# A diffusion block on one core: tables in the slots of split weights, four slots of each kind, and the last attention head inside the output projection

## The chip, the cores and the metric

The kernel runs on one NeuronCore of a Trainium2 chip. The metric is the device time of one execution in microseconds (us). TensorE (PE) does the matmuls, VectorE (DVE) and ScalarE (ACT) the elementwise work, GpSimd (POOL) a few elementwise steps, and SyncE (SP) issues most DMAs. Each engine works through its own instructions in a fixed order and waits for the others by semaphores.

## The reference

Two streams of 256 tokens with 1024 channels, the latent stream `lat` and the context stream `cx`, pass through two layers. Each layer is a gated feed-forward block (ffn), a mixer and a second ffn; each of them reads a normed and modulated copy of the stream (`adaln_in`) and adds its result to it through a gate. The mixer of layer 0 is the one that the change touches:

```python
def macaron(h, gain, mod, k, w1, w3, w2):
    return h + 0.5 * mod[:, 3*k+2] * swiglu(adaln_in(h, gain, mod, k), w1, w3, w2)

# layer 0: mixer_ab
u = h @ w_in                                # q, k, v of 4 heads, and 3 x 512 channels for hyena
a = head_out(diff_attend(q, k_all, v_all, lam))   # two softmaxes a head, subtracted, then rmsnorm
b = hyena(u[..., 3 * A_WIDTH:])             # short convolution, then two long ones by FFT, each gated
y = concatenate([a, b], axis=-1) @ w_out    # 512 channels of each
```

Layer 1 has neighbourhood attention with 16 heads in its place. All of it is float32.

## The kernel before

**Matmuls in three parts.** Every operand of a matmul is split into a high part `h` in fp32r and the rest `l`; `mm3` (L161 to L164) adds three matmuls, high by high (L162), high by low (L163) and low by high (L164). A piece of weights is 128x1024 elements: `whalf` takes one slot of tag `whi` and one of tag `wlo` in the pool `wp` and calls `split` (L156), in which ACT writes the high part (L158) and DVE, or POOL where it is asked for, subtracts it for the low part (L159). So a piece is there once both have run, and its two slots come free when the last matmul that reads them is done. The pool holds three slots of each tag; the raw weights come by DMA into `raw`, three slots too.

**Where pieces stand in line.** A block of an ffn needs four pieces: two of `w1` and two of `w3`. `ffn` begins with `ffn_first`, which asks for all four at once and puts the low parts on POOL (on DVE in the very first ffn, whose pieces are made early); `products` then runs them over stream 0 and, when it is normed, over stream 1. `project_first` does the same at the start of a mixer, with four pieces in `mixer_ab`, by DVE. With three slots the fourth piece waits until the first is read for the last time. All other places (`project`, `project_v`, `out_project`, the later blocks of an ffn) use pieces by twos.

**Norms.** Before each block a stream's statistics go squares on ACT, six adds on DVE (L448), four matmuls (L452, L453), a power on POOL (`rs`, L456), a broadcast by matmul (L464), then `xr` and `h` on DVE and ACT (L491 to L493).

**mixer_ab.** It loads three tables of the Fourier transforms, each 128 x 2 x 512 (4 KB a partition, the size of one slot of a piece), into a pool `tb` of their own. `project` runs over the channels of `w_in`, two pieces at a time; `step()` pulls the next part of the generator `convolutions` between them. `head(hd)` does one attention head: scores (L752), two softmaxes for each half of the queries (`softmax_exp`, then L758), transposes of the result on PE (L677), and the product with the values (`pu<-ah,v`). For stream 0 a score is 512 wide, for stream 1 256 wide. `conv2` (`ps<-tab,y`) ends the convolution and fills `zb`, four tiles. `norms` norms two heads: squares, L903, a power on POOL (`rs16`, L907), L912, and `za`, the tiles `z`. Then `out_project` adds the product with `w_out`: eight blocks of output from `zb` (96 matmuls 512 wide, `pd<-zb`), and then the same from `za` (`pd<-z`).

**Order.** The order of each engine's instructions is fixed when the program is built, by a list scheduler; a pool's slots enter it as dependencies: a tile can be written only after the last reader of the tile that had its slot. So the order of the code sets priorities, and the number of slots sets what may run early.

Of the kernel before, what the change touches and what calls it, by code (L numbers as in the profile page):

```python
# [18 lines left out]
P = 128  # L19
# [85 lines left out]
def tile_dit(ctx: ExitStack, tc: tile.TileContext, a: dict, out: bass.AP, dbg=None):  # L105
# [1 line left out]
    dbg = dbg or {}  # L107

    const = ctx.enter_context(tc.tile_pool(name="const", bufs=1))
    wp = _Pool(ctx.enter_context(tc.tile_pool(name="wp", bufs=3)))  # L110
    hp = _Pool(ctx.enter_context(tc.tile_pool(name="hp", bufs=8)))
    gp = _Pool(ctx.enter_context(tc.tile_pool(name="gp", bufs=10)))
    mp = _Pool(ctx.enter_context(tc.tile_pool(name="mp", bufs=6)))
    fp = _Pool(ctx.enter_context(tc.tile_pool(name="fp", bufs=3)))
    tb = _Pool(ctx.enter_context(tc.tile_pool(name="tb", bufs=3)))
    tp = _Pool(ctx.enter_context(tc.tile_pool(name="tp", bufs=NT)))
    xp = _Pool(ctx.enter_context(tc.tile_pool(name="xp", bufs=6)))
    sp = _Pool(ctx.enter_context(tc.tile_pool(name="sp", bufs=2)))
# [392 lines left out]
    def gates(l, i, half):  # L511
        g = sp.tile([P, 8, 2], F32, tag="gate", name="gate")
        V.tensor_scalar(g, modT[l][:, 8 * i : 8 * i + 8, :], 0.5 if half else 1.0, None, op0=ALU.mult)
        return g
# [173 lines left out]
    def mixer_ab(ad, mods, after):  # L688
# [49 lines left out]
        def head(hd):  # L738
            (qh, ql), (kh, kl) = qk[hd], qk[4 + hd]
            if hd % 2 == 0:  # L740
                oT[hd], oT[hd + 1] = G(F32, "oT")
            for s in range(2):
                nk = 4 if s == 0 else 2
                n = P * nk
                at = [PS() for _ in range(nk // 2)]
                for qt in range(2):
                    qs = slice(LAT * s + P * qt, LAT * s + P * qt + P)
                    pss = [PU(), PU()]
                    for i in range(3):
                        for m in range(2):  # L750
                            pr = slice(64 * m, 64 * m + 64)
                            nc.tensor.matmul(pss[m][:, :n], (qh, qh, ql)[i][pr, qs], (kh, kl, kh)[i][pr, TOK - n :],  # L752
                                             start=i == 0, stop=i == 2)
                    e0, s0 = softmax_exp(pss[0], n)
                    e1, s1 = softmax_exp(pss[1], n)
                    V.tensor_tensor(s1[:, 3:4], s1[:, 2:3], nlam, op=ALU.mult)
                    S.activation(e1[:, :n], e1[:, :n], AF.Copy, scale=s1[:, 3:4])
                    V.scalar_tensor_tensor(e0[:, :n], e0[:, :n], s0[:, 2:3], e1[:, :n], op0=ALU.mult, op1=ALU.add)  # L758
                    transposed(at, e0, nk, qt)
                po = PU()  # L760
                hs = slice(P * hd, P * hd + P)
                weighted(po, at, nk, lambda kt: [x[:, hs] for x in vs[kt + 4 - nk]])
                S.activation(oT[hd][:, LAT * s : LAT * s + LAT], po[:, :LAT], AF.Copy)
# [126 lines left out]
        def step(n=1):  # L890
            for _ in range(n):
                next(hyena, None)
# [3 lines left out]
        def norms(hds):  # L896

            st = PS()
            for i, hd in enumerate(hds):
                q = T(name="sq")  # L900
                S.activation(q, oT[hd], AF.Square)
                for t in range(4):
                    nc.tensor.matmul(st[:, 4 * i + t : 4 * i + t + 1], q[:, P * t : P * t + P], ones, start=True, stop=True)  # L903
            n = 4 * len(hds)
            rs = sp.tile([P, 16], F32, tag="rs16", name="rs16")
            V.tensor_scalar(rs[:, :n], st[:, :n], 1.0 / P, EPS, op0=ALU.mult, op1=ALU.add)
            nc.gpsimd.tensor_tensor(rs[:, :n], rs[:, :n], nhalf[:, :n], op=ALU.pow)  # L907
            for i, hd in enumerate(hds):
                bc = PS()
                for t in range(4):  # L910
                    k = 4 * i + t
                    nc.tensor.matmul(bc[:, P * t : P * t + P], rs[:, k : k + 1].to_broadcast([P, P]), ident, start=True, stop=True)  # L912
                x = T(name="on")
                V.scalar_tensor_tensor(x, oT[hd], sub8, bc, op0=ALU.mult, op1=ALU.mult)
                za.append(G(name="z"))
                split(*za[hd], x)

        tab = [tb.tile([P, 2, TOK], F32R, tag="tb", name="tab") for i in range(3)]
        tables(0, 3, lambda i: tab[i][:, 0], lambda i: tab[i][:, 1])
        tabs = [[tab[0][:, x].rearrange("p (i t f) -> p i t f", i=2, t=2)[:, i] for x in range(2)] for i in range(2)]  # L920
        inv = [[[tab[1 + f][:, x, LAT * i : LAT * i + LAT] for x in range(2)] for i in range(2)] for f in range(2)]
# [14 lines left out]
        project_v(win, 1280, h, emit_v(1), PD)  # L936
        step(2)
        head(2)
        step()
        head(3)  # L940
        step(99)
        norms((2, 3))
        gate = gates(0, 5, False)
        out_project(wout, range(4, 8), [(x[:, 0], x[:, 1]) for x in zb], gate, [0, 1])
        mods(-1)
        out_project(wout, range(4), za, gate, [0, 1], None, after)

    def mixer_c(ad, mods, after):
# [174 lines left out]
    def mods(ns, first=None, until=None):  # L1123

        def f(b, part=0):
            if b < 0:
                if first:
                    mod_until(*first)  # L1130
            elif b < NFB - 2:
                mod_some(ns[part])
            elif b == NFB - 2 and until and part == 3:
                mod_until(*until)
        return f
# [47 lines left out]
```

## Time and profile before

| what | value |
|---|---|
| median of 3 runs | 1936.07 us (1931.74 to 1936.6) |
| the profiled execution | 1930.48 us, span 1928.7 us |
| PE busy | 1845.0 us, 96% of the span |
| DVE busy | 1281.3 us, 66% |
| ACT busy | 732.4 us, 38% |
| POOL busy | 91.1 us, 5% |
| PE's mean granted clock | 0.98 of full speed |

The profile gives the busy time of each engine, with matmuls counted from start to modelled end, and PE's granted clock. There are two levels of it, 2.4 GHz (1.0) and 1.2 GHz (0.5). A 128x512 matmul that stands in a row follows the last by about 0.23 us at the full level, a 128x256 one by 0.12 us, and by twice that at the lower level. The span falls into an opening of 60 us, the first ffn (to about 445 us), `mixer_ab` (to about 745), two ffns (to 1130 and 1510), layer 1's mixer (to about 1720) and the last ffn.

### The profile page before, as it was taken

How to read it: one execution, taken by the hardware profiler on the slowest of the kernel's cores; microseconds unless marked ns; L12 is line 12 of the kernel's file. 1: busy time of each engine (PE TensorE's matmuls, PEld its weight loads, DVE VectorE, ACT ScalarE, POOL GpSimd, SP SyncE). 2: the span in 40 equal slices, each digit the busy share in tenths (PEclk: the TensorE clock that was granted, in tenths of full speed). 3: DMA queues.
4: the chain of work that ended last, by engine and by line, in shares of the span. 5: the costliest groups of instructions: out<-in, count | busy, mean ns of one | idle time of the engine just before them, and what ended most of it. 6: DMA issues, size and time to landing. Idle time of an engine off the chain costs nothing.

```text
span 1928.7 us, 25545 instructions
## 1 busy us (share of the span) xinstructions
PE 1845.0 (96%) x10250; PEld 1561.9 (81%) x10250; DVE 1281.3 (66%) x2007; ACT 732.4 (38%) x1191; POOL 91.1 (5%) x91
## 2 busy tenths in 40 slices
PE   7899999998998888999999999999999999979998
PEld 3678788888887667878888888888888988879998
DVE  5567686677898656677767467566334866667675
ACT  4333233234454433422322333223212566644444
POOL 1000000000101002000000010000000101110000
PEclk9999999999999889999999999999999999989999
DMA  8664455451332111555545315434323233325552
GB/s 282 223 228 175 144 217 178 141 185 47 119 99 66 55 44 44 189 182 186 175 153 177 129 45 202 169 142 141 100 88 114 78 83 104 83 88 204 182 184 88
DMA packets 182791, 266.63 MB, mean 138 GB/s; under 512 B 19026, under 2 KB 133973, under 8 KB 182673
## 3 DMA queue, kind: packets, MB, share of 16 engines
q1 hardware_dynamic: 179128, 256.35, 39.7%
q0 software_dynamic: 2288, 6.53, 1.0%
q10 hardware_dynamic: 1256, 2.13, 0.3%
q8 instruction: 80, 1.31, 0.3%
q14 instruction: 39, 0.31, 0.0%
HBM read 259.74 MB, written 5.24 MB: 137 GB/s over the span
## 4 chain that ended last, share of the span: by engine, by line
PE 56%; DVE 2%; ACT 1%; POOL 1%; issue 1%; DVEq 0%; POOLq 0%; ACTq 0%
PE pu L164 11%; PE pu L162 10%; PE pu L163 10%; PE pd L162 5%; PE pd L163 5%; PE pd L164 5%; PE ps L162 2%; PE ps L164 2%; PE ps L163 2%; PE pu L1034 1%; POOL wl L159 1%; DVE acc L448 1%; PE pu L1004 1%; PE ps L307 1%; ACT wh L158 0%
## 5 line engine op out<-in xcount | busy, mean ns | idle before, releaser
L164 PE MATMUL pu<-h,wl 128*128 128x512 f32 (+1 forms) x1600 | 549.1, 344 | 15.6 <-POOL wl L159 10.9
L162 PE MATMUL pu<-h,wh 128*128 128x512 f32 (+1 forms) x1600 | 548.7, 345 | 6.5 <-ACT h L492 3.1
L163 PE MATMUL pu<-h,wh 128*128 128x512 f32 (+1 forms) x1600 | 548.6, 343 | 0.2 <-DVE h L493 0.2
L158 ACT ACTIVATE wh<-raw 128x1024 fp32r<-128x1024 f32 x228 | 241.2, 1059 | 598.1 <-PE pu L163 403.0
L159 DVE TENSOR_TENSOR wl<-raw,wh 128x1024 fp32r<-128x1024 f32 x216 | 264.1, 1224 | 171.9 <-ACT wh L158 170.9
L164 PEld LDWEIGHTS pu<-h,wl 128*128 128x128 f32 x1600 | 307.4, 192 | 51.7 <-POOL wl L159 11.8
L162 PEld LDWEIGHTS pu<-h,wh 128*128 128x128 f32 x1600 | 306.5, 192 | 51.4 <-ACT wh L158 8.0
L163 PEld LDWEIGHTS pu<-h,wh 128*128 128x128 f32 x1600 | 307.7, 192 | 35.2 <-issue 0.8
L296 DVE SCALAR_TENSOR_TENSOR mv<-mw,kept,mv 128x1024 f32<-128x1024 f32 x210 | 258.2, 1278 | 2.6 <-DMA mw<-in_mod_w_dram 2.6
L556 DVE TENSOR_TENSOR sg<-sg,pu 128x512 f32<-128x512 f32 (+1 forms) x87 | 52.5, 604 | 173.0 <-PE pu L164 153.9
L158 ACT ACTIVATE w<-raw 128x1024 fp32r<-128x1024 f32 x88 | 90.9, 1055 | 188.8 <-PE ps L163 110.5
L519 DVE SCALAR_TENSOR_TENSOR kept<-pd,gate,kept 128x256 f32<-128x256 f32 x244 | 110.5, 478 | 58.8 <-PE pd L164 58.4
L159 DVE TENSOR_TENSOR w<-raw,w 128x1024 fp32r<-128x1024 f32 x88 | 106.6, 1221 | 43.4 <-ACT w L158 43.1
L162 PE MATMUL pd<-g,w 128*128 128x512 f32 (+1 forms) x376 | 133.2, 354 | 0.0
L164 PE MATMUL pd<-g,w 128*128 128x512 f32 (+1 forms) x376 | 132.2, 352 | 0.0
L163 PE MATMUL pd<-g,w 128*128 128x512 f32 (+1 forms) x376 | 132.2, 352 | 0.0
L162 PE MATMUL ps<-g,w 128*128 128x512 f32 (+1 forms) x320 | 116.1, 363 | 0.0
L164 PE MATMUL ps<-g,w 128*128 128x512 f32 (+1 forms) x320 | 116.0, 363 | 0.0
L163 PE MATMUL ps<-g,w 128*128 128x512 f32 (+1 forms) x320 | 116.0, 363 | 0.0
L162 PE MATMUL pd<-h,wh 128*128 128x512 f32 (+1 forms) x288 | 108.3, 376 | 2.3 <-ACT bo L423 1.2
L163 PE MATMUL pd<-h,wh 128*128 128x512 f32 (+1 forms) x288 | 107.3, 372 | 0.0
L164 PE MATMUL pd<-h,wl 128*128 128x512 f32 (+1 forms) x288 | 107.2, 372 | 0.0
(284 smaller groups left out, 2724.0 us busy)
## 6 DMA issues: line engine op xcount, KB each, us to landing
raw<-in_ffn_w_dram SPq DMA_DIRECT2D x132, 1024.0 KB, 5.3
mw<-in_mod_w_dram SPq DMA_DIRECT2D x144, 512.0 KB, 5.8
raw<-in_ab_w_in_dram SPq DMA_DIRECT2D x12, 1024.0 KB, 4.9
raw<-in_na_w_in_dram SPq DMA_DIRECT2D x12, 1024.0 KB, 5.9
raw<-in_ab_w_out_dram SPq DMA_DIRECT2D x4, 1024.0 KB, 5.9
raw<-in_na_w_out_dram SPq DMA_DIRECT2D x4, 1024.0 KB, 5.0
bias<-in_na_rpb_dram SPq DMA_DIRECT2D x32, 96.0 KB, 6.2
raw<-in_x_dram SPq DMA_DIRECT2D x1, 1024.0 KB, 5.1
```

The costliest lines, as they stand in the source:

```text
L158: S.activation(hi, src, AF.Copy)
L159: eng.tensor_tensor(lo, src, hi.bitcast(F32), op=ALU.subtract)
L162: nc.tensor.matmul(ps, wh, xh, start=start, stop=False)
L163: nc.tensor.matmul(ps, wh, xl, start=False, stop=False)
L164: nc.tensor.matmul(ps, wl, xh, start=False, stop=stop)
L296: V.scalar_tensor_tensor(acc, mw, c, acc, op0=ALU.mult, op1=ALU.add)
L307: nc.tensor.matmul(ps[32 * j : 32 * j + 32], row[:, 31 - b : 63 - b], mod_acc[l, i][j % 2][:, j // 2], start=b == 0, stop=b == len(batch) ...
L448: V.tensor_tensor(acc, acc, q, op=ALU.add)
L519: V.scalar_tensor_tensor(res[d][:, sl], ps[:, po], g[:, d, s : s + 1], res[d][:, sl], op0=ALU.mult, op1=ALU.add)
L556: V.tensor_tensor(sg[:, sl], sg[:, sl], p3[:, sl], op=ALU.mult)
L1004: nc.tensor.matmul(pss[m], x[pr, qsl], y[pr], start=n == 0, stop=n == 2)
L1034: nc.tensor.matmul(po[:, LAT * m : LAT * m + LAT], w, x[:, sl], start=kt == 0 and n == 0, stop=kt == 3 and n == 1)
```

## The change

- The pool `wp` gets four slots of `whi` and four of `wlo` in place of three and three (`raw` keeps three).
- The pool `tb` is gone. The three tables take slots of `wp`: `tab[0]` one of `whi`, `tab[1]` and `tab[2]` two of `wlo`. From the loading of the tables until the last matmul of `conv2` three slots of `whi` and two of `wlo` are left to the weights.
- At the end of `mixer_ab` the last parts of the convolution are pulled before head 3, and head 3 is written between the two halves of the projection of `zb`, in a function that `out_project` calls after each half (`b or head(3)` runs it after the first). `norms((2, 3))` comes after that projection. `mods(-1)`, which does nothing here, is dropped.

```diff
-    wp = _Pool(ctx.enter_context(tc.tile_pool(name="wp", bufs=3)))
+    wp = _Pool(ctx.enter_context(tc.tile_pool(name="wp", bufs=4)))
...
-    tb = _Pool(ctx.enter_context(tc.tile_pool(name="tb", bufs=3)))
...
-        tab = [tb.tile([P, 2, TOK], F32R, tag="tb", name="tab") for i in range(3)]
+        tab = [wp.tile([P, 2, TOK], F32R, tag=("whi", "wlo", "wlo")[i], name="tab") for i in range(3)]
...
         step(2)
         head(2)
-        step()
-        head(3)
         step(99)
+        gate = gates(0, 5, False)
+        out_project(wout, range(4, 8), [(x[:, 0], x[:, 1]) for x in zb], gate, [0, 1], lambda b: b or head(3))
         norms((2, 3))
-        gate = gates(0, 5, False)
-        out_project(wout, range(4, 8), [(x[:, 0], x[:, 1]) for x in zb], gate, [0, 1])
-        mods(-1)
         out_project(wout, range(4), za, gate, [0, 1], None, after)
```

A line of the changed kernel has the number before less one (L752 becomes L751, L677 becomes L676, `mm3` L161 to L163).

PE, the first two softmaxes of head 3, that is its scores 512 wide (`pu<-qk`) and the transposes that wait for the softmaxes (`ps<-kept,e`). In the kernel before PE has the end of the scores, four of twelve matmuls of `zb`, and the transposes:

```order
L162 MATMUL pd<-zb,wh 128x512
L163 MATMUL pd<-zb,wh 128x512
L752 MATMUL pu<-qk 128x512 x6
L164 MATMUL pd<-zb,wl 128x512
L162 MATMUL pd<-zb,wh 128x512
L163 MATMUL pd<-zb,wh 128x512
L164 MATMUL pd<-zb,wl 128x512
L677 MATMUL ps<-kept,e 128x128 x8
```

In the changed kernel PE has at the same place:

```order
L162 MATMUL pd<-zb,wh 128x512
L163 MATMUL pd<-zb,wl 128x512
L751 MATMUL pu<-qk 128x512 x11
L676 MATMUL ps<-kept,e 128x128 x8
L161 MATMUL pu<-ah,v 128x256
L751 MATMUL pu<-qk 128x256 x6
```

Before, the twelve matmuls of `zb` stood among the scores and ahead of the transposes; now they, and the rest of `conv2`, stand ahead of the scores, and the transposes follow the scores directly.

PE, the second two softmaxes of head 3 (scores 256 wide) and their transposes. In the kernel before:

```order
L752 MATMUL pu<-qk 128x256 x6
L677 MATMUL ps<-kept,e 128x128 x2
L752 MATMUL pu<-qk 128x256 x3
L162 MATMUL ps<-tab,y 128x256
L163 MATMUL ps<-tab,y 128x256
```

In the changed kernel PE has, behind 36 matmuls of `zb` that follow the six scores shown above:

```order
L162 MATMUL pd<-zb,wh 128x512
L163 MATMUL pd<-zb,wl 128x512
L163 MATMUL pu<-ah,v 128x256
L676 MATMUL ps<-kept,e 128x128 x2
L751 MATMUL pu<-qk 128x256 x6
L161 MATMUL pd<-zb,wh 128x512
L162 MATMUL pd<-zb,wh 128x512
```

Here the transposes stood right behind the scores, and now 36 matmuls of `zb` stand between; 19 more stand ahead of the next transposes. In all 84 of the 96 matmuls of `zb` stand behind the first transposes of head 3, as before, but behind them all come the norm's L902 (L903 before), six matmuls of `z`, and the norm's L911 (L912 before), where 70 matmuls of `zb` stood behind L912.

DVE, the start of `mixer_ab`: `h` of stream 1 for its last two blocks of channels, then low parts of weights (`wl`), and `cv`, the short convolution of the first results. In the kernel before the low part here, `wl_3546`, is the fourth piece's (the third's, `wl_3542`, stands 69 rows above):

```order
L493 SCALAR_TENSOR_TENSOR h_3354<-xr_3489,kept_96,h_3354 128x256
L493 SCALAR_TENSOR_TENSOR h_3359<-xr_3493,kept_96,h_3359 128x256
L159 TENSOR_TENSOR wl_3546<-raw_3539,wh_3545 128x1024
L777 SCALAR_TENSOR_TENSOR cv_3745<-pu_3549,kept_96,cv_3745 128x2x255
L777 SCALAR_TENSOR_TENSOR cv_3762<-pu_3550,kept_96,cv_3762 128x2x255
```

In the changed kernel DVE has `wl_3539`, the third piece's, and `wl_3543`, the fourth's:

```order
L492 SCALAR_TENSOR_TENSOR h_3351<-xr_3486,kept_93,h_3351 128x256
L492 SCALAR_TENSOR_TENSOR h_3356<-xr_3490,kept_93,h_3356 128x256
L158 TENSOR_TENSOR wl_3539<-raw_3536,wh_3538 128x1024
L158 TENSOR_TENSOR wl_3543<-raw_3536,wh_3542 128x1024
L776 SCALAR_TENSOR_TENSOR cv_3742<-pu_3546,kept_93,cv_3742 128x2x255
```

The third piece's low part has moved from the time before stream 1's norm to behind it, next to the fourth's. On PE 46 matmuls of stream 0 stand ahead of stream 1's L451 there, where 72 stood ahead of L452. On POOL the order of the four low parts ahead of the second ffn and the norms' powers was one, `rs`, two, `rs`, one, and is two, `rs`, two, `rs`; and on PE 66 matmuls of that ffn's first block stand ahead of the broadcast L463 of stream 1, where 51 stood ahead of L464.

## Rows read from the trace of the kernel before

**Rows 1.** Windows, columns in the first row: an ffn's steady blocks, then `mixer_ab`.

```profile
core 0: us, PE busy (x) PEld busy (x) DVE busy (x) ACT busy (x) POOL busy (x), PEclk, DMA share, GB/s
165.00:420.00 255.00, 255.00 (x1135) 206.48 (x1134) 179.80 (x213) 74.48 (x87) 0.55 (x1) 1.00 0.51 180
420.00:745.00 325.00, 295.07 (x1707) 251.91 (x1706) 237.62 (x473) 144.92 (x291) 27.66 (x36) 0.95 0.22 74
```

**Rows 2.** What PE waits for: us in total, times, longest.

```profile
PE ps L677 <- DVE e L758: 15.1, 8, 5.0
PE pu L164 <- POOL wl L159: 10.9, 5, 4.1
```

**Rows 3.** Timeline of PE, heads 2 and 3: start, us, instruction, [idle before <-releaser].

```profile
646.01 1.65 PE L752 MATMUL pu<-qk 64*128 64x512 f32 x12
652.71 1.11 PE L677 MATMUL ps<-kept,e 128*128 128x128 f32 x4 [5.05 <-DVE e L758]
654.58 1.11 PE L677 MATMUL ps<-kept,e 128*128 128x128 f32 x4 [0.76 <-DVE e L758]
...
676.71 0.66 PE L677 MATMUL ps<-kept,e 128*128 128x128 f32 x4 [0.92 <-DVE e L758]
678.93 0.66 PE L677 MATMUL ps<-kept,e 128*128 128x128 f32 x4 [1.56 <-DVE e L758]
...
687.12 0.44 PE L677 MATMUL ps<-kept,e 128*128 128x128 f32 x2 [2.62 <-DVE e L758]
```

**Rows 4.** The same view: where the two heads' norm reaches PE.

```profile
701.04 1.34 PE L912 MATMUL ps<-kept,rs 128*128 128x128 f32 x5 [1.26 <-POOL rs L907]
```

**Rows 5.** Windows, as rows 1: head 2, head 3, matmuls of `z` 512 wide.

```profile
646.00:671.00 25.00, 15.44 (x82) 12.44 (x83) 14.20 (x35) 11.63 (x28) 0.00 (x0) 0.73 0.12 43
671.00:694.00 23.00, 16.86 (x86) 12.94 (x84) 12.10 (x33) 11.21 (x30) 0.00 (x0) 0.85 0.00 1
721.00:731.00 10.00, 10.00 (x46) 8.29 (x45) 6.39 (x12) 2.76 (x5) 0.00 (x0) 1.00 0.22 68
```

**Rows 6.** Timeline of PE: waits for a piece's low part, at four first blocks.

```profile
79.75 0.39 PE L164 MATMUL pu<-h,wl 128*128 128x256 f32 x1 [0.76 <-DVE wl L159]
...
752.26 0.51 PE L164 MATMUL pu<-h,wl 128*128 128x256 f32 x1 [4.05 <-POOL wl L159]
...
762.68 0.58 PE L164 MATMUL pu<-h,wl 128*128 128x256 f32 x1 [1.15 <-POOL wl L159]
...
779.21 0.39 PE L164 MATMUL pu<-h,wl 128*128 128x256 f32 x1 [1.93 <-POOL wl L159]
...
1162.23 0.39 PE L164 MATMUL pu<-h,wl 128*128 128x256 f32 x1 [1.82 <-POOL wl L159]
...
1737.16 0.38 PE L164 MATMUL pu<-h,wl 128*128 128x256 f32 x1 [1.93 <-POOL wl L159]
```

**Rows 7.** Windows, as rows 1: behind the fourth piece's wait at 779 us.

```profile
780.00:786.00 6.00, 6.00 (x41) 6.00 (x40) 2.96 (x3) 1.53 (x3) 0.00 (x0) 0.74 0.97 343
```

**Rows 8.** Timeline of POOL: a low part ahead of the second ffn.

```profile
747.22 4.98 POOL L159 TENSOR_TENSOR wl<-raw,wh 128x1024 fp32r<-128x1024 f32 x1 [4.08 <-ACT wh L158]
```

**Rows 9.** Timeline of DVE around 1712 us, while POOL splits from 1710.90 on.

```profile
1710.48 0.41 DVE L448 TENSOR_TENSOR acc<-acc,sq 128x256 f32<-128x256 f32 x1
...
1711.20 2.36 DVE L448 TENSOR_TENSOR acc<-acc,sq 128x256 f32<-128x256 f32 x1
1713.48 0.47 DVE L519 SCALAR_TENSOR_TENSOR kept<-pd,gate,kept 128x256 f32<-128x256 f32 x1
```

**Rows 10.** Timeline of PE, start of `mixer_ab`.

```profile
457.42 0.35 PE L452 MATMUL ps<-kept,acc 128*128 128x1 f32 x2 [0.89 <-DVE acc L448]
...
462.29 1.01 PE L162 MATMUL pu<-h,wh 128*128 128x256 f32 x3 [1.53 <-ACT h L492]
```

**Rows 11.** Groups of DVE instructions from 460 to 646 us: xcount, busy us, mean ns.

```profile
L159 DVE TENSOR_TENSOR wl<-raw,wh 128x1024 fp32r<-128x1024 f32 x19 | 23.2, 1220 | 10.9 <-ACT wh L158 10.5
```

**Rows 12.** Windows, as rows 1: the busiest stretch of DVE in `mixer_ab`.

```profile
500.00:540.00 40.00, 40.00 (x199) 33.98 (x199) 36.66 (x66) 17.29 (x31) 7.33 (x11) 1.00 0.36 119
```

## The prediction

> **What bounds the kernel now.** I read the busy shares by stretch first. In the steady blocks of an ffn PE is busy for 255.00 of 255 us at the full clock [rows 1]: a slot more can't help there, since nothing waits for a piece. Between 420 and 745 us it is busy for 295.07 of 325 at a mean clock of 0.95 [rows 1], so 30 us of idle PE and some 16 us of clock lie in this tenth of the program. Then I read what PE waits for: 15.1 us for the softmax of the heads, in eight waits, and 10.9 us for the low part of a piece from POOL, in five [rows 2]. These two waits are what the change touches, the first by head 3, the second by the fourth slot. So PE is the bound, and the change can win only where PE stands still or where it runs at the lower clock because it stood still. The sums are made on the profiled execution, 1930.48 us, which lies 5.6 us under the median of the three runs; I carry the difference over to the median, 1936.07.
>
> **Part 1, a fourth slot at the first block of an ffn.** The fourth piece had to wait until the first was read for the last time, and PE waited for its split: 0.76 us in the first ffn (by DVE), then, by POOL, 1.93, 1.82 and 1.93 us [rows 6], at 79.75, 779.21, 1162.23 and 1737.16. With four slots it takes a slot that the stage before gave back, and each of these waits goes; what is late next is the norm of stream 1, which the order still puts ahead of most of this block. Behind the wait at 779 us the clock fell: 6 us at a mean of 0.74 [rows 7], that is 6 x 0.26 = 1.6 us. The others show no such dip that I would count. In the second ffn the wait of 4.05 us at 752.26 [rows 6] stays: it is a piece whose slot the projection of `z` holds until about 746, and POOL then takes 4.98 us for it [rows 8]; now the third piece has that place. But with more pieces at hand 66 matmuls stand ahead of stream 1's broadcast where 51 did, so 15 x 0.12 = 1.8 us of work moves into time in which PE stood (a matmul 256 wide takes 0.12 us; the wait of 1.15 us at 762.68 [rows 6] is part of that time). The fourth split is no new work; it moves on POOL's queue ahead of the power `rs` of stream 1, where the third stood before, so the queue is no longer there. Sum of part 1: -0.8 (first ffn), -1.9 - 1.6 - 1.8 = -5.3 (second), -1.8 (third), -1.9 (fourth): **-9.8 us**; bounds -12 and -4, the latter if the earlier splits hold DVE in two places.
>
> That bound comes from a row: while POOL splits, one add of the norm took 2.36 us where it takes 0.41, and an update of `kept` from PSUM in the same time took 0.47, as always [rows 9]. So a split that now runs while the first half of `z` is evicted costs nothing, and one that runs beside a norm's adds costs some 2 us; two such adds and a third of the same kind make the bound. I take none, because the splits that run beside adds stay the same in number.
>
> **Part 2, head 3 within the projection of `zb`.** In the first pair of softmaxes PE waited 0.92 and 1.56 us, with twelve matmuls of `zb` ahead of them. These now stand ahead of the scores, and the transposes follow directly, as in head 2, where PE waits 5.05 and 0.76 us [rows 3]. So this wait grows, by up to 5.81 - 2.48 = 3.3 us; I take 2.8, since the first scores of head 3 are still issued a little early. In the second pair PE waited 2.62 us [rows 3]; 36 matmuls of `zb` now cover it, 36 x 0.22 = 7.9 us by the row of ten us with 46 matmuls [rows 5]: -2.6. The clock: from 671 to 694 us it was 0.85 [rows 5], 23 x 0.15 = 3.4 us lost, in several dips, one for each wait. Now one longer wait is followed by a dense row of `zb`; I take one dip less in the head and one less at the norm: -3.0 (bounds 0 and -5). Head 2 stays. At the end, the norm of heads 2 and 3: PE waited 1.26 us for POOL's power [rows 4] and had 70 matmuls of `zb` behind the broadcast, which hid the scaling and splitting of `z`. Now six matmuls of `z`, 1.3 us, stand ahead of the broadcast and six behind. The nearest row for the exposed part is the wait of 1.53 us between a broadcast and the first `h` at 462.29 [rows 10], the same sort of chain; against 1.3 us of cover and the old 1.26 I charge 0.8 (bounds 0 and 3). Sum: 2.8 - 2.6 - 3.0 + 0.8 = **-2.0 us**; bounds -6 and +3.
>
> **Part 3, the tables in the slots.** At the start of `mixer_ab` only two pieces are whole. 46 matmuls of stream 0 stand ahead of stream 1's statistics, where 72 did. Those came 0.89 us too late for PE already [rows 10], so 26 x 0.12 = 3.1 us of work moves behind the norm, that is, onto the path: stream 1 can't start sooner than at 462.29 or a little before (DVE has one split less there, 1.22 us [rows 11], but table splits as well; I take 0.6). The third and fourth low parts then follow the last matmul of the first two: a split of 1.22 us, of which I charge 0.8 beyond the wait for the old fourth piece. Sum 3.1 - 0.6 + 0.8 = **+3.3 us**; bounds 0 and +6, the latter if the longer wait drops the clock for longer.
>
> Behind that, to 646 us, DVE makes 19 low parts `wl` of 1.22 us [rows 11] and four of the values', with two slots instead of three. A piece is 24 matmuls 512 wide, 24 x 0.22 = 5.3 us. By the order most have at least one whole piece between the release of their slot and their first use, and 5.3 us against 1.22 leaves 4 us. Three stand closer: the first behind the opening four pieces and the second low part of each of the two values' projections, with some 1.6 to 1.8 us of matmuls between. I charge 0.5 us each: **+1.5 us**; bounds 0 and +10. The tables' DMAs and their splits are the same; only their slots are others.
>
> **The sum.** -9.8 - 2.0 + 3.3 + 1.5 = -7.0 us: 1923.5 for the profiled execution, 1929 for the median.
>
> **Rivals.**
> *Slower, two slots are too few.* Wherever DVE is more than 4 us behind when a slot comes free, the split comes too late, and PE waits; and while DVE stands at a split whose slot isn't free, its queue stands too: the convolution's spectra, the evictions of the projections. For it: DVE is busy for 36.66 of 40 us between 500 and 540 us [rows 12], so it has little to catch up with. Against it: PE has no idle time at all in that stretch. If the lateness costs one split's 1.22 us at sixteen pieces, that is 19.5 in place of 1.5: -7.0 + 18.0 = +11, 1947 us. It turns slower from 10 us on.
> *The gains are eaten.* Splits of POOL meet the norm's adds at the second and the last ffn, +4 by [rows 9], and the start of `mixer_ab` costs its upper bound, +2.7: -0.3 in all, 1936 us. For it: POOL's split took 4.98 us at the very place [rows 8]. Against: the last ffn's splits that met the adds before are the same two. The Trainium skill, page "SBUF — State Buffer", section "Who interferes with whom", has a rule that speaks for this rival: a DVE instruction with two inputs in SBUF and a GpSimd instruction that reads SBUF shut each other out, and the later one stands for the whole length of the other. The add of 2.36 us and the eviction of 0.47 [rows 9] agree with it. By it a fourth split beside the adds, `xr` and `h` of stream 1 would hold DVE for its whole 2.4 us wherever the two meet; the sum above has no such meeting that was not there before, and the rival has two.
> *Better.* The clock stays up behind head 3's first wait, the norm hides, two slots cost nothing: -6 - 10 + 2.5 = -13.5, 1922 us.
> *The projection of `zb` doesn't hide anything*, because the scheduler's order on PE isn't met by DVE: part 2 is +3, 1934 us, within the "eaten" case's reach.
>
> **How the numbers follow.** The forecast has a chance of 0.45, from 1925 to 1934; better 0.18; eaten, or nothing hidden, 0.21; slower 0.16. A measurement of this kernel can tell about 0.3%, 5.8 us, from no change: faster means under 1930.3, slower over 1941.9. Of the forecast 0.28 falls under it, with the better case 0.46; same gets 0.37, slower 0.17. For 8 in 10 the range leaves out most of the slower case and the far end of the better one: 1916 to 1943.
>
> **What would show it.** In the changed trace the waits for a low part at 79, 779, 1162 and 1737 us should be gone, and the one of about 4 us at 752 should be there, a few us earlier. Head 3's first transposes should wait some 5 us, its later ones not at all, and the row of `zb` should run at clock 1.0. At the start of `mixer_ab` stream 1's statistics should be waited for some 3 to 4 us, and no wait for `wl` should appear to 646 us except at three places. I am wrong if `wl` from DVE appears among PE's larger waits there, or if the norm's adds take 2 us at two more places.

## The result, and the profile after

The changed kernel takes 1923.93 us (median of 4 runs, 1923.49 to 1925.58), the kernel before beside it 1934.93: a ratio of 0.9947, with a 95% interval of 0.9929 to 0.9964. That is 10 to 11 us faster, where 7 were forecast. The profiled execution has a span of 1921.5 us, 7.2 less than that of before; the profiled execution of before lies 4.5 us under its median, so the two traces hold some 7 of the 11 us. The page's first row says that PE still bounds all; what it lost is idle time, 72.1 us of the span where it was 83.7.

```profile
PE 1849.4 (96%) x10250; PEld 1562.8 (81%) x10250; DVE 1277.9 (67%) x2007; ACT 732.2 (38%) x1191; POOL 90.5 (5%) x91
```

What PE waits for (us in total, times, longest), to be read beside [rows 2]:

```profile
PE ps L676 <- DVE e L757: 10.7, 3, 4.8
...
PE pu L163 <- DVE wl L158: 5.0, 3, 2.1
PE pd L161 <- DVE kept L518: 4.8, 4, 2.3
...
PE ps L676 <- DVE smx L669: 3.8, 1, 3.8
...
PE pu L163 <- POOL wl L158: 1.9, 1, 1.9
```

POOL's low parts, 10.9 us in five waits before, are 1.9 in one. The heads' transposes waited 15.1 us in eight and wait 10.7 + 3.8 in four: fewer waits, hardly shorter in sum.

The program falls into stages between events that both traces have (the first matmul of a kind, a norm's broadcast on PE). This table is worked out from their starts on PE's timeline:

| stage | before | after | difference | forecast |
|---|---|---|---|---|
| start to the first ffn's first matmul | 54.6 | 57.0 | +2.4 | 0 |
| first ffn, first block | 30.7 | 30.3 | -0.5 | -0.8 |
| first ffn, rest, to `mixer_ab`'s first broadcast | 359.7 | 361.0 | +1.3 | 0 |
| from there to the convolution's first transposes | 34.7 | 39.9 | +5.1 | +3.3 |
| from there to head 2 | 166.2 | 169.7 | +3.5 | +1.5 |
| head 2 to the second ffn's first broadcast | 97.2 | 93.6 | -3.6 | -2.0 |
| second ffn, first block | 43.1 | 35.5 | -7.6 | -5.3 |
| second ffn, rest | 345.7 | 346.1 | +0.4 | 0 |
| third ffn, first block | 35.8 | 32.7 | -3.1 | -1.8 |
| third ffn, rest, and `mixer_c` | 552.4 | 549.4 | -3.0 | 0 |
| last ffn, first block | 19.6 | 16.3 | -3.3 | -1.9 |
| from there to the end | 188.8 | 190.0 | +1.2 | 0 |

The first row is no effect of the change: in the kernels below, that stretch takes 54.2 to 59.2 us whatever they change. The four first blocks together have 14.5 us less, where 9.8 were forecast; the two stages that the tables' slots touch have 8.6 us more, where 4.8 were; and 3 us came in `mixer_c`, for which nothing was forecast.

Timeline of PE after (start, us, instruction, [idle before <-releaser]), the places of [rows 3, 4, 6, 10]: `mixer_ab`'s start, heads 2 and 3, and the second ffn's first block.

```profile
458.57 0.39 PE L163 MATMUL pu<-h,wl 128*128 128x256 f32 x1 [1.75 <-DVE wl L158]
467.40 0.79 PE L161 MATMUL pu<-h,wh 128*128 128x256 f32 x2 [1.53 <-ACT h L491]
...
664.30 1.97 PE L676 MATMUL ps<-kept,e 128*128 128x128 f32 x8 [4.84 <-DVE e L757]
...
675.41 0.66 PE L676 MATMUL ps<-kept,e 128*128 128x128 f32 x2 [3.84 <-DVE smx L669]
...
695.87 1.97 PE L676 MATMUL ps<-kept,e 128*128 128x128 f32 x8 [4.10 <-DVE e L757]
...
758.53 0.39 PE L163 MATMUL pu<-h,wl 128*128 128x256 f32 x1 [1.87 <-POOL wl L158]
769.64 0.81 PE L463 MATMUL ps<-kept,rs 128*128 128x128 f32 x4 [1.13 <-POOL rs L455]
```

In head 3 one wait of 4.10 us stands where waits of 0.92, 1.56, 2.62 and a smaller one stood [rows 3]; its second pair of softmaxes, behind the matmuls of `zb`, isn't waited for at all. The fourth piece's waits of [rows 6] are gone at all four places. At the second ffn the wait of 4.05 us has shrunk to 1.87, and this is one reason why that block gained more than was forecast: POOL's split there took 3.01 us, not 4.98 as in [rows 8].

```profile
755.47 3.01 POOL L158 TENSOR_TENSOR wl<-raw,wh 128x1024 fp32r<-128x1024 f32 x1 [4.08 <-ACT wh L157]
```

### The profile page after: what moved, and what is told of

Same layout as the page of the kernel before. It is cut to its first block, busy times and chain, and to the rows that moved or that the text cites. A ratio compares the mean times of both kernels' runs of the same rounds, so it can differ in the third digit from the quotient of the medians.

```text
span 1921.5 us, 25514 instructions
## 1 busy us (share of the span) xinstructions
PE 1849.4 (96%) x10250; PEld 1562.8 (81%) x10250; DVE 1277.9 (67%) x2007; ACT 732.2 (38%) x1191; POOL 90.5 (5%) x91
## 3 DMA queue, kind: packets, MB, share of 16 engines
q1 hardware_dynamic: 179128, 256.35, 39.9%
## 4 chain that ended last, share of the span: by engine, by line
PE 58%; DVE 2%; ACT 1%; issue 1%; POOL 1%; DVEq 0%; ACTq 0%
PE pu L161 10%; PE pu L163 10%; PE pu L162 10%; PE pd L161 6%; PE pd L163 5%; PE pd L162 5%; PE ps L161 2%; PE ps L163 2%; PE ps L162 2%; PE pu L1030 1%; PE ps L306 1%; PE pu L1000 1%; DVE acc L447 1%; POOL wl L158 0%; PE ps L676 0%
## 5 line engine op out<-in xcount | busy, mean ns | idle before, releaser
L163 PE MATMUL pu<-h,wl 128*128 128x512 f32 (+1 forms) x1600 | 549.5, 344 | 7.0 <-DVE wl L158 5.0
L161 PE MATMUL pu<-h,wh 128*128 128x512 f32 (+1 forms) x1600 | 548.6, 345 | 6.2 <-ACT h L491 3.9
L161 PEld LDWEIGHTS pu<-h,wh 128*128 128x128 f32 x1600 | 307.1, 193 | 50.4 <-ACT wh L157 5.7
L163 PEld LDWEIGHTS pu<-h,wl 128*128 128x128 f32 x1600 | 308.0, 193 | 43.5 <-DVE wl L158 6.0
L161 PE MATMUL pd<-g,w 128*128 128x512 f32 (+1 forms) x376 | 133.2, 354 | 0.0
L163 PE MATMUL pd<-g,w 128*128 128x512 f32 (+1 forms) x376 | 132.4, 352 | 0.0
L161 PE MATMUL ps<-g,w 128*128 128x512 f32 (+1 forms) x320 | 116.2, 363 | 0.0
L163 PE MATMUL ps<-g,w 128*128 128x512 f32 (+1 forms) x320 | 116.0, 363 | 0.0
L161 PE MATMUL pd<-h,wh 128*128 128x512 f32 (+1 forms) x288 | 108.7, 377 | 2.1 <-ACT u L961 0.9
L163 PE MATMUL pd<-h,wl 128*128 128x512 f32 (+1 forms) x288 | 107.5, 373 | 1.2 <-DVE wl L158 1.2
```

The source lines that it names most:

```text
L161: nc.tensor.matmul(ps, wh, xh, start=start, stop=False)
L163: nc.tensor.matmul(ps, wl, xh, start=False, stop=stop)
```

## The experiments

The theory: (1) the fourth slot removes the fourth piece's waits, and moves splits away from the norms; (2) head 3 within the projection trades a few short waits for one long one and gains little; (3) the tables' slots starve the start of `mixer_ab`. The rivals: the gain hangs on head 3; the loss in `mixer_ab` is the scheduler's other order and not the slots; `mixer_c`'s gain is chance.

### One part at a time

The kernel before with the new end of `mixer_ab` alone:

```diff
         head(2)
-        step()
-        head(3)
         step(99)
+        gate = gates(0, 5, False)
+        out_project(wout, range(4, 8), ..., gate, [0, 1], lambda b: b or head(3))
         norms((2, 3))
...
```

> The kernel before with only the end of mixer_ab in the new order (head 3 within the projection of zb, its norm behind it); three slots of each kind and the tables in their own pool. Theory, from the changed trace: this edit alone is worth the stretch from head 2 to the second ffn's first broadcast, 97.2 us before and 93.6 after, so about -3.5 us, 0.998 of the time before, and nothing elsewhere. Rival: the gain in that stretch comes from the slots (the four pieces of the projections ready earlier), then the stretch stays at 96 to 97 us and the time does not move. Second rival: the two parts need each other, and this one alone is slower, because the norm of heads 2 and 3 is exposed.

Measured: 1935.89 us against 1937.27, ratio 1.0001 (0.9989 to 1.0013, ten runs). Alone, the edit can't be told from no change.

The changed kernel with the old end:

```diff
         head(2)
+        step()
+        head(3)
         step(99)
+        norms((2, 3))
         gate = gates(0, 5, False)
-        out_project(wout, range(4, 8), ..., gate, [0, 1], lambda b: b or head(3))
-        norms((2, 3))
+        out_project(wout, range(4, 8), ..., gate, [0, 1])
...
```

> The changed kernel with the end of mixer_ab in the old order: four slots and the tables in them, head 3 ahead of the projection of zb. Theory: the first blocks of the ffns win some 12 us and the end of mixer_c 4 to 5, the slots that the tables hold cost 8 to 9, so about -7 to -8 us, 0.996 of the time before. Rival: all of the measured gain hangs on head 3, then this is as the kernel before. From the start of mixer_ab to head 2 it should be as slow as the changed kernel (39.9 us from the first broadcast to the first transposes of the convolution, 169.7 from there to head 2).

Measured: 1927.13 us, ratio 0.9954 (0.9939 to 0.9969, ten runs). The slots carry the gain; the rival that head 3 does is out. Windows from head 2 to the second ffn's first broadcast, of before, of head 3's edit alone, of the slots alone and of the changed kernel (columns as in [rows 1]):

```profile
646.00:743.20 97.20, 78.01 (x410) 64.58 (x409) 53.84 (x115) 35.60 (x78) 4.71 (x3) 0.88 0.13 44
```

```profile
652.40:748.20 95.80, 78.73 (x409) 65.62 (x408) 52.90 (x115) 35.14 (x78) 5.56 (x3) 0.84 0.14 44
```

```profile
657.30:754.60 97.30, 79.29 (x410) 66.53 (x409) 55.33 (x115) 35.48 (x78) 7.11 (x4) 0.88 0.13 44
```

```profile
657.80:751.40 93.60, 76.68 (x409) 64.35 (x408) 54.90 (x115) 34.89 (x78) 7.95 (x4) 0.87 0.14 46
```

With the slots the edit is worth 97.3 - 93.6 = 3.7 us in this stretch, without them 1.4, at a lower clock (0.84). The idle time of PE falls by 2.1 us without the slots (97.2 - 78.0 = 19.2 and 95.8 - 78.7 = 17.1) and by 1.1 with them (18.0 and 16.9). The rest is busy time of the same matmuls, 0.7 us more without the slots and 2.6 less with them. On time the kernel with the slots alone isn't told from the changed one (0.9954 and 0.9947).

### Which slots are short

Five low slots, so that `mixer_ab` has three of each kind left. Memory for slots and tables is then as before the change.

```diff
-        lo = wp.tile([P, *shape], F32R, tag="wlo", name=name + "l")
+        lo = wp.tile([P, *shape], F32R, tag="wlo", bufs=5, name=name + "l")
...
-        tab = [wp.tile(..., tag=("whi", "wlo", "wlo")[i], name="tab") for i in range(3)]
+        tab = [wp.tile(..., tag=("whi", "wlo", "wlo")[i], bufs=(4, 5, 5)[i], name="tab") for i in range(3)]
```

> The changed kernel with five slots of wlo in place of four, so that mixer_ab has three slots of each kind left as the kernel before. The memory for slots and tables is then as before the change. Theory (two low slots are what costs the 8.6 us from the start of mixer_ab to head 2): the stretch from the first broadcast to the transposes of the convolution goes back from 39.9 to some 35 us, the next one from 169.7 to 166 or 167, and the time falls by 5 to 9 us against the changed kernel, to about 1916 to 1919 us. Rival: the loss there is the scheduler's other order, or stream 1's statistics, and not the slots; then nothing moves.

Measured: 1911.78 us, ratio 0.9881 (0.9864 to 0.9899). The kernel is 10 to 12 us faster than the changed one, more than the 5 to 9 of the theory. The changed one was run again beside the later ones:

> The changed kernel itself again, to stand beside the next three on one chip: some 1924 us, 0.994 to 0.996 of the time before. Every theory expects the same waits as in its first trace (1.9 us for a piece's low part ahead of the second ffn, 4.1 us at head 3's first transposes); where its clock falls may differ.

Measured: 1921.88 us, ratio 0.9933 (0.9916 to 0.995); its stages are those of the first trace within 0.6 us.

From the first broadcast to the transposes five low slots take 35.8 us in place of 39.9: 4.1 of the 5.1 lost come back, so this loss is the slots'. The next stage, to head 2, falls from 169.7 to 168.6 only, 1.1 of 3.5. That is no measure of the slots there, as the windows show, of before, of the changed kernel and with five low slots:

```profile
479.80:646.00 166.20, 160.61 (x870) 134.24 (x868) 138.86 (x261) 79.08 (x155) 21.55 (x31) 0.99 0.28 92
```

```profile
488.20:657.80 169.60, 161.60 (x869) 132.77 (x868) 140.53 (x263) 81.04 (x158) 22.14 (x31) 0.99 0.27 91
```

```profile
482.10:650.70 168.60, 163.07 (x870) 136.33 (x868) 139.63 (x261) 80.42 (x156) 21.32 (x31) 0.97 0.27 91
```

PE is idle for 5.6, 8.0 and 5.5 us: the 2.4 us that the tables' slots cost come back in full, and the lower clock of this trace hides it. All traces agree: idle 7.4 to 9.9 us in the six of kernels with two slots of a kind left there, 5.4 to 5.6 in the eight with three. The stage itself takes 166.2 to 169.0 us in kernels with the code of before there, by the clock alone.

The first blocks and the stages behind fall too: the second ffn's first block by 3.0 us and head 2 to the broadcast by 1.7, with waits that are nearly those of the changed kernel, so that part of the 10 us is again the clock. PE at the start of `mixer_ab` with five low slots:

```profile
456.57 0.39 PE L163 MATMUL pu<-h,wl 128*128 128x256 f32 x1 [1.75 <-DVE wl L158]
463.44 0.71 PE L463 MATMUL ps<-kept,rs 128*128 128x128 f32 x4 [0.52 <-POOL rs L455]
475.23 0.38 PE L161 MATMUL pu<-h,wh 128*128 128x256 f32 x1 [0.37 <-ACT wh L157]
476.49 0.39 PE L163 MATMUL pu<-h,wl 128*128 128x256 f32 x1 [0.76 <-DVE wl L158]
```

The wait of 1.75 us for the second piece is there too; the wait of 1.53 us for `h` of stream 1 isn't, since a third piece covers it. The windows show the clock's part, of before, of the changed kernel, then with five low slots:

```profile
445.10:479.80 34.70, 29.97 (x220) 28.60 (x221) 25.17 (x57) 15.23 (x32) 0.69 (x1) 0.90 0.10 31
```

```profile
448.30:488.20 39.90, 34.61 (x223) 32.41 (x224) 23.90 (x54) 13.89 (x31) 0.69 (x1) 0.83 0.16 54
```

```profile
446.30:482.10 35.80, 31.13 (x222) 28.82 (x223) 26.70 (x57) 15.23 (x32) 0.69 (x1) 0.95 0.18 60
```

Idle 4.7, 5.3 and 4.7 us: the waits are nearly the same in sum, and the difference is busy time of the same matmuls, 30.0, 34.6 and 31.1 us, at a granted clock of 0.90, 0.83 and 0.95. The other traces show the same gap: 38.4 to 39.9 us with two slots left, 34.5 to 35.9 with three.

The tables in two high slots and one low one, to tell whether it is the low slots or any two:

```diff
-        tab = [wp.tile(..., tag=("whi", "wlo", "wlo")[i], name="tab") for i in range(3)]
+        tab = [wp.tile(..., tag=("whi", "whi", "wlo")[i], name="tab") for i in range(3)]
```

> The changed kernel with the tables in two slots of whi and one of wlo, so that mixer_ab has two high slots and three low ones left, in place of three and two. Theory (a piece needs one of each, so two pieces at a time is the limit whichever kind is short): from mixer_ab's first broadcast to the transposes of the convolution 39 to 41 us, as the changed kernel's 39.9, and the time as the changed kernel's within 3 us. Rival (the low slots are scarce because DVE's splits are late in its line, and ACT, which writes the high parts, has time): the stretch goes back towards 36 us, as with five low slots, and the time falls by 3 us or more.

Measured: 1924.25 us, ratio 0.9952 (0.9937 to 0.9967); the stretch takes 38.9 us. So the time is the changed kernel's, and a piece lacks whichever kind is short. The rival that low slots are special is out.

Five low slots with the old end of `mixer_ab`:

```diff
         head(2)
+        step()
+        head(3)
         step(99)
+        norms((2, 3))
         gate = gates(0, 5, False)
-        out_project(wout, range(4, 8), ..., gate, [0, 1], lambda b: b or head(3))
-        norms((2, 3))
+        out_project(wout, range(4, 8), ..., gate, [0, 1])
...
```

> Five slots of wlo and four of whi, the tables in them, and the end of mixer_ab in the old order. Theory (the slots carry the whole gain, and head 3's place is worth 0 to 3 us): 1912 to 1916 us, at most 3 us over the kernel with five low slots and the new order (1911.8). Rival (head 3's place is worth much once no wait in mixer_ab hides it): 1918 us or more.

Measured: 1919.24 us, ratio 0.9922 (0.9897 to 0.9948). On this base head 3's place is worth some 6 to 7 us (6.7 in the stage below, 5.6 on time against the next kernel, which was run beside it), more than I expected. The rival's number came; its reason isn't shown. From head 2 to the broadcast, old end, then new:

```profile
648.10:746.80 98.70, 80.06 (x409) 66.89 (x408) 54.36 (x114) 35.59 (x78) 7.11 (x4) 0.86 0.13 43
```

```profile
650.70:742.70 92.00, 75.37 (x410) 62.71 (x409) 53.84 (x114) 34.94 (x78) 7.95 (x4) 0.87 0.15 46
```

The idle time is 18.6 and 16.6 us, 2 apart as without the slots. The other 4.7 us are busy time of the same matmuls. The mean granted clock hardly differs (0.86 and 0.87), but by the trace's clock records 24.4 us of PE's busy time lie at the lower level with the old end and 18.4 with the new, which is worth (24.4 - 18.4) / 2 = 3.0 of the 4.7. So in each of the three pairs of traces the edit takes 1 to 2 us of waits away, and with the clock it came to anything from nothing to 7.

Head 2's norm ahead of the projection of `zb`, with five low slots:

```diff
+        norms((2,))
         gate = gates(0, 5, False)
         out_project(wout, range(4, 8), ..., gate, [0, 1], lambda b: b or head(3))
-        norms((2, 3))
+        norms((3,))
```

> Five slots of wlo, the new order, and head 2's norm ahead of the projection of zb, so that only head 3's stands between it and the projection of z. Theory (the norm behind the projection is exposed: PE waited 1.4 us for POOL's power with six matmuls of z as cover, and the broadcasts of both heads stand there): nine more matmuls of z can cover the power, the wait of 1.4 us goes, -1 to -2 us against 1911.8. Rival: the wait for head 3's power is the same, since POOL takes as long for four columns as for eight, and the order on PE does not use the cover; then no change within 2 us.

Measured: 1913.64 us, ratio 0.9889 (0.9872 to 0.9907), no change. The wait for the power fell from 1.40 to 0.81 us, but not by the cover: in both kernels six matmuls of `z` stand between the norm's L902 and its L911. POOL's power is shorter, 1.91 us for four columns and 2.50 for eight, and that is the 0.6 us. The first line is from five low slots, the second from this kernel:

```profile
716.62 2.50 POOL L906 TENSOR_TENSOR rs<-rs,kept 128x8 f32<-128x8 f32 x1 [72.85 <-DVE rs L905]
```

```profile
714.62 1.91 POOL L906 TENSOR_TENSOR rs<-rs,kept 128x4 f32<-128x4 f32 x1 [37.53 <-DVE rs L905]
```

So the rival was right that the order on PE doesn't use the cover, and wrong that POOL takes as long for four columns.

### Where POOL's splits stand

Three slots from `mixer_c` to the end (tags of their own), all else as changed:

```diff
+    tags = ["whi", "wlo", 4]
...
+    tags[:] = ["whj", "wlj", 3]
     mixer_c(ads[1, 1], none, then(1, 2))
```

> The changed kernel, but from mixer_c to the end only three slots of each kind. Theory (the fourth slot also lets the pieces ahead of the last ffn be split earlier, so that POOL's splits meet fewer of the norm's adds): the 4.8 us that the stretch from mixer_c's first broadcast to the last ffn's won go back, and the fourth piece's wait of 1.9 us returns, so +6 to +8 us against the changed kernel, about 1931 us. Rival: the stretch of mixer_c is shorter for another reason (chance, or another order in the attention); then only the 2 to 3 us of the last ffn's first block come back.

Measured: 1926.51 us, ratio 0.9955 (0.9939 to 0.997, ten runs): 2 to 3 us over the changed kernel by the medians, which the intervals don't tell apart, and not the 6 to 8 of the theory. In its trace `mixer_c` takes 208.3 us and the last first block 18.8, nearly as before the change (209.0 and 19.6, against 204.4 and 16.3 after), but the third ffn's rest is 2.1 us shorter than in the changed kernel, and the end 1.2: 3.3 us in all. The 2.1 us are no gain: 19 matmuls 256 wide that stood ahead of the broadcast between the two stages stand behind it here, and `mixer_c` has them. The two together take 551.2 us, 549.4 in the changed kernel and 552.4 before. The norm's old stall is back, so this part of `mixer_c`'s gain was not chance. First the stall before, then here on PE and POOL:

```profile
1713.88 2.17 DVE L448 TENSOR_TENSOR acc<-acc,sq 128x256 f32<-128x256 f32 x1
...
1717.36 0.59 PE L452 MATMUL ps<-kept,acc 128*128 128x1 f32 x2 [5.04 <-DVE acc L448]
```

```profile
1714.78 0.59 PE L451 MATMUL ps<-kept,acc 128*128 128x1 f32 x2 [5.05 <-DVE acc L447]
...
1708.32 4.86 POOL L158 TENSOR_TENSOR wl<-raw,wh 128x1024 fp32r<-128x1024 f32 x2 [1.60 <-DVE acc L447]
```

In the changed kernel POOL has one split at that place instead of two, and PE waits 2.28 us:

```profile
1705.26 0.95 DVE L447 TENSOR_TENSOR acc<-acc,sq 128x256 f32<-128x256 f32 x2 [0.15 <-ACT sq L445]
...
1706.59 2.37 POOL L158 TENSOR_TENSOR wl<-raw,wh 128x1024 fp32r<-128x1024 f32 x1 [1.54 <-ACT wh L157]
...
1707.21 2.56 DVE L447 TENSOR_TENSOR acc<-acc,sq 128x256 f32<-128x256 f32 x2 [0.15 <-ACT sq L445]
...
1710.61 0.39 PE L161 MATMUL pd<-z,wh 128*128 128x256 f32 x1 [2.28 <-DVE kept L518]
```

Then DVE in POOL's place. First only ahead of the last ffn, with five low slots:

```diff
-        ws = ws or ffn_first(l, j, nc.gpsimd)
+        ws = ws or ffn_first(l, j, V if (l, j) == (1, 1) else nc.gpsimd)
```

> Five slots of wlo, the new order, and the low parts of the last ffn's first four pieces by DVE in place of POOL. Theory (a split on POOL holds the norm's adds on DVE for its length: two adds took 2.6 us in the changed kernel, and PE waited 2.3 us for an eviction behind them): the adds take 0.4 us each, but DVE does four splits of 1.22 us itself, three of them before the adds; from mixer_c's first broadcast to the last ffn's -1 to +1 us, the time unmoved within 2 us. If POOL's split is the whole cause of that wait, the stretch is shorter by about 2 us; if it grows by 2 us or more, POOL was the right engine for it.

Measured: 1908.63 us (1907.46 to 1916.83), ratio 0.9878 (0.9848 to 0.9908): not told from five low slots alone. `mixer_c` is 1.6 us shorter in the traces. Then ahead of all three, with five low slots:

```diff
-        ws = ws or ffn_first(l, j, nc.gpsimd)
+        ws = ws or ffn_first(l, j)
```

> Five slots of wlo, the new order, and the low parts ahead of the second, third and fourth ffn all by DVE in place of POOL. Theory (POOL's split takes 2.4 to 3 us where DVE's takes 1.2, and it holds DVE meanwhile): PE's wait of 1.9 us for the third piece's low part ahead of the second ffn falls to under 1, the eviction that waited 1.9 us behind a split at the projection of z comes at once, but DVE does twelve splits more, 14.6 us, partly beside the norm's adds: -4 to 0 us against 1911.8. Rival (DVE is the norm's engine and the adds stand behind the splits): the broadcasts come later, and the time is 2 us or more over 1911.8.

Measured: 1902.83 us (1901.16 to 1906.36), ratio 0.9838 (0.9821 to 0.9854): 9 us under five low slots, more than the theory's 0 to 4, and the fastest of all, 30 us under the kernel before. The five stages from head 2 to the last ffn's first block fall by 9.3 us in sum. The same edit on the kernel before and on the changed one:

> The kernel before, with the low parts ahead of the second, third and fourth ffn by DVE in place of POOL; slots, tables and head 3 as before. Theory (part of what the fourth slot wins is that POOL's splits move away from the norm's adds; where DVE splits, there is nothing to move away from): the stretch of mixer_c falls from 209.0 to some 205 to 206 us without a fourth slot, the fourth piece's waits of 1.8 to 1.9 us fall to about 0.8, as in the first ffn; -5 to -10 us, 0.995 to 0.997 of the time before. Rival (POOL's splits matter only for the third piece at the second ffn): -2 us, not to be told from no change.

Measured: 1919.06 us, ratio 0.9912 (0.9886 to 0.9939), more than the theory expected. The kernel before gains 16 us by this edit alone; by the ratios that is more than by the change (0.9947 and 0.9933), but the intervals overlap. Its second ffn's first block falls from 43.1 to 34.4 us and `mixer_c` from 209.0 to 205.0, without a fourth slot. PE's wait of 1.9 us for an eviction that stood behind POOL's split, first below, is gone; in that projection PE waits 0.37 us, further on, and the fourth piece's wait at the last ffn is 0.76:

```profile
735.56 0.39 PE L162 MATMUL pd<-z,wh 128*128 128x256 f32 x1 [1.90 <-DVE kept L519]
```

```profile
743.20 0.38 PE L162 MATMUL pd<-z,wh 128*128 128x256 f32 x1 [0.37 <-DVE kept L519]
...
1726.31 0.38 PE L164 MATMUL pu<-h,wl 128*128 128x256 f32 x1 [0.76 <-DVE wl L159]
```

> The changed kernel with the same low parts by DVE. Theory (slots and the engine of the splits add up, less what both remove): -5 to -8 us against the changed kernel, 1914 to 1918 us, 0.990 to 0.992 of the time before. Rival (the fourth slot has already removed what POOL's splits cost): within 3 us of the changed kernel.

Measured: 1912.35 us, ratio 0.988 (0.9847 to 0.9913): the two add up in part. Of the change's 11 us, some 7 are left (1919.06 to 1912.35) once DVE makes the splits.

## Why the prediction came out right, point by point

**The direction and the sum.** 1929 was forecast and 1923.9 measured, inside the range of 1916 to 1943; faster held. The three parts went the way that was said, and the first is the one that decides, as the kernel with the slots alone shows (0.9954 against 0.9947). That the sum came so near is partly luck. Against the forecast, part 1 gave 4.7 us more, part 2 1.6 more and `mixer_c` 3.0 that weren't forecast, while part 3 cost 3.8 more and stages that no part speaks of 5.3: together the traces' -7.2 beside the forecast's -7.0. The median lies 1 us under the 1925 to 1934 of the forecast, next to the better case (whose -13.5 makes 1922.6, not 1922), and not by that case's reasons: the clock didn't stay up behind head 3's first wait, and two slots cost more than was charged, not nothing.

**Part 1, the fourth slot.** -9.8 forecast, -14.5 in the four first blocks. The fourth piece's waits fell away at each place, and the sum was too small. Mis-sized was the step "the wait of 4.05 us stays": the third piece has that place now, as was said, but its split took 3.01 us and the wait 1.87. Seven more matmuls stand ahead of it, which is 0.8 us of the 2.2, and the split was held for less: before, three groups of DVE's `xr` and `h` ran while it was under way and only then one stood beside it for long (two `h` in 2.58 us); after, only one group ran first, and the next one stood (three `h` in 3.37 us where they take 1.27). The kernel before with DVE's splits shows what hung on POOL there: 8.7 us of that block, 5.3 of them idle time of PE and the rest the clock. The step "I take none, because the splits that run beside adds stay the same in number" failed in `mixer_c`: with the fourth slot each split runs one piece earlier, one split meets the adds instead of two, and PE's 5.04 us wait became 2.28. With three slots from there on it came back at 5.05. So the rival that POOL's splits eat the gain was wrong in its sign: moving them was part of the gain.

The adds of the changed kernel show the meeting: a pair of them takes 0.95 us alone and 2.56 us beside POOL's split. With this the rule agrees that was cited for the rival, in the Trainium skill, page "SBUF — State Buffer", section "Who interferes with whom": a GpSimd instruction that reads SBUF and a DVE instruction with two inputs in SBUF shut each other out. By it an edit that takes splits off POOL frees DVE as well. The kernel before gained 16 us by such an edit, with twelve more splits on DVE, but not by this alone: POOL's split is also the longer one, 2.4 us undisturbed against DVE's 1.22. The rows show both. At the end of `mixer_c` two adds took 2.36 and 2.17 us beside POOL's splits and some 0.4 each without, which is 3.7 of PE's 5.04 us; the fourth piece's wait at the last ffn, with no add beside the split, fell from 1.93 to 0.76 us, which is the shorter split. No run parts the two over the whole time.

**Part 2, head 3.** -2.0 forecast, -3.6 in the trace. The first pair of softmaxes grew from 2.48 to 4.10 us, not by 2.8; the second pair's wait went, as forecast; the norm's wait is 1.40 us. On time the edit alone is 1.0001 (0.9989 to 1.0013), so that between -2.1 and +2.5 us all is open; with five low slots it is 6 to 7 us. The sum came near by luck: its waits were +1.0 (2.8 - 2.6 + 0.8) and its clock -3.0, and the trace has 2.2 us less idle time and 1.3 less busy time. The step "one dip of the clock less" was a guess at the part that varies most; the mean granted clock of the stage is 0.88 before and 0.87 after.

**Part 3, the tables' slots.** +4.8 forecast, +8.6 measured. At the start the cost is the slots', as five low slots show, but the mechanism was half wrong. I looked for 3 to 4 us of wait at the statistics. PE waited nowhere for them; it waited 1.75 us for the second piece's low part, which DVE makes behind stream 0's norm, and then for `h` and the third piece, and the clock was at its lower level for longer: 0.83 over the stretch, where it was 0.90 before. That wait is the sign of being wrong that was named, but only at the start, and five low slots have it too, so the order of the code makes it and not the shortage. The step that failed there is the one that put 26 matmuls, 3.1 us, on the path as time in which PE stands: idle time rose by 0.6 us only, busy time by 4.6, and the wait of 1.53 us for `h` stood there before as well. The bound of +6 was set for that. Later, 2 us more than forecast: of the 3.5 us 2.4 are idle time, which goes with five low slots and is there in every trace with two slots left, where +1.5 was forecast; the rest is busy time, and the same code of before took up to 2.8 us more in other traces by the clock. The rival "two slots are too few" came in small only: between the convolution's start and head 2 PE's largest waits are for `y` (2.3 us, where it waited 2.1 before) and the softmax (1.74, where it waited 0.66), and only 0.6 us for a low part of the values. So most of the cost isn't where I charged it, at three low parts: by the waits, other results of DVE and ACT come later.

**What stays open.** The third ffn's rest takes 345.1 to 346.2 us in kernels with four slots or more and 343.0 to 343.4 in those with three behind it. With three slots from `mixer_c` on it is the place of the broadcast that ends the stage, as said; in the kernel before as many matmuls 256 and 512 wide stand ahead of it as in the changed one, so it isn't that, and what it is wasn't tried. Nor does any run show what decides where the clock falls.

## What to carry to other kernels

A slot more in a ring of tiles paid here where a consumer asks for as many tiles at once as the ring holds plus one, at four first blocks, and where it moved a split away from a norm's adds, and not in the steady blocks. Tables that borrow slots of the ring take part of that gain back, most at the place where all slots are asked for, and here it didn't matter which kind they borrowed; count what is left while they are alive. Before giving a second engine work to relieve the first, look at what the first does while the second runs: here POOL's help cost more than it gave, and taking it away was worth as much as the change's slots, or more.

## What the runs showed of the hardware

The same waits can cost different times by the clock. The second ffn's first block has the same waits, 1.9 and 1.1 us, in the changed kernel and with five low slots, and takes 35.5 and 32.5 us:

```profile
751.40:787.00 35.60, 32.51 (x237) 31.55 (x237) 18.89 (x43) 13.42 (x30) 6.22 (x3) 0.90 0.32 104
```

```profile
742.70:775.20 32.50, 29.45 (x236) 28.48 (x236) 18.85 (x43) 13.39 (x30) 6.23 (x3) 1.00 0.36 114
```

PE is idle for 3.1 us in each; in the first the granted clock fell to the lower level twice, in the second not at all. With head 2's norm moved it was 35.5 again, the waits unchanged, and with DVE's splits ahead of the last ffn 32.5. So a stage with the same waits of 1 to 2 us can differ by 3 us, and I had treated each dip as the price of its wait.
